# Row sums on one Trainium2 core: the first load becomes a whole group of 16 rows per partition

## The chip, the cores and the metric

The kernel runs on one core of one Trainium2 chip. The metric is device time in microseconds (us): the median of the timed runs. Times inside the kernel come from one profiled execution, counted from its first instruction.

## The reference

```python
batch, seq, dim = 32, 512, 1024
# x: (32, 512, 1024) float32
np.sum(x, axis=-1)          # -> (32, 512) float32
```

16384 rows of 1024 numbers are each summed to one number: 67.1 MB are read and 0.07 MB written.

## The kernel before

**Layout.** The 16384 rows are spread over 128 partitions, 128 rows for each. They lie in two regions: region A, the first 2048 rows, holds 16 rows per partition, and region B holds the other 112 per partition. In each, the rows of one partition are contiguous in memory. `rows_from(j, n)` names rows j to j+n-1 of all partitions. `BIG` is 16 rows per partition, a group of 8.39 MB (64 KB in each partition), so there are 8 groups, 0 to 7; group 0 is region A. `last` is 7 and `tail` is 112, the first row of the last group. `FIRST` is 8.

**Loads.** There are three buffers of 16 rows per partition. The first load is the first eight rows of the last group (4.19 MB, 32 KB per partition). It goes to buffer 0 by SP's queue (L97), and `issue_first_load_at_entry` moves its instruction to the very start of the program, ahead of the barrier that the other engines pass. Groups 0 to 6 follow on POOL's queue (L99), 8.39 MB each, to buffers 1, 2, 0, 1 and so on. The first two of them wait for nothing. Each later one waits until `summed` shows that the reduction of the load three places earlier has ended, which frees the buffer. The prediction numbers loads from 0 (the first one), so load 3 is the first that waits. The last eight rows of the last group are loaded in four runs (two into buffer 2, two into `ends`) behind the same kind of wait.

**Sums.** DVE takes the loads in the order of their issue: for each it waits for the landing and runs one `tensor_reduce` (`vec`, L106), which raises `summed`. The last full group is shared: ten rows go to DVE (`halves`, L115) and six to ACT (`act`, L135). The runs of the last eight rows follow in the same manner. ACT stores the sums that are ready early (L210, L211), and SP the last ones (L227), once DVE and ACT are done.

**Order.** No scheduler takes part: each engine runs its instructions as the program gives them, and only semaphores tie them together. SP issues one load and the last store, POOL all other loads, so a wait on POOL also holds the loads behind it.

Of the kernel before, what the change touches and what calls it, by code (L numbers as in the profile page):

```python
# [30 lines left out]
def kernel(  # L31
# [5 lines left out]
    nc = tc.nc  # L37
# [12 lines left out]
    BIG = 16  # L50
# [15 lines left out]
    def rows_from(j, n):  # L66
        if j < ONE:
            return x_a[:, j : j + n, :]
        return x_b[:, j - ONE : j - ONE + n, :]

    last = J // BIG - 1
    tail = last * BIG
    FIRST = 8

    bufs = [
        ctx.enter_context(nc.sbuf_tensor(f"rows_{k}", [P, BIG * dim], fp32))
        for k in range(3)
    ]
# [9 lines left out]
    def semaphore(name):  # L88
        return ctx.enter_context(nc.semaphore(name=name))

    def block_of(t, a, n):
        return t[:, a * dim : (a + n) * dim].rearrange("p (n d) -> p n d", d=dim)

    def load(dst, src, k):
        sem = semaphore(f"load_{k}")
        if k == "first":
            nc.sync.dma_start(out=dst, in_=src).then_inc(sem, 16)  # L97
        else:
            nc.gpsimd.dma_start(out=dst, in_=src, single_packet=True).then_inc(sem, 16)  # L99
        return sem  # L100

    summed = semaphore("summed")
# [40 lines left out]

    t = bufs[0]
    block = block_of(t, 0, FIRST)
    landed = load(block, rows_from(tail, FIRST), "first")
    loads = [(landed, tail, block)]
    for g in range(last):  # L150
        t = bufs[(1 + g) % 3]
        if g > 1:
            nc.gpsimd.wait_ge(summed, g - 1)
        block = block_of(t, 0, BIG)
        loads.append((load(block, rows_from(g * BIG, BIG), g), g * BIG, block))

    j = tail + FIRST
    t = bufs[(1 + last) % 3]
# [25 lines left out]
    landed, first, block = loads[-1]  # L188
# [70 lines left out]
```

## Time and profile before

| | |
|---|---|
| median of 3 timed runs | 160.72 us (160.71 to 160.88) |
| profiled execution, first to last instruction (its span) | 159.6 us |
| median less span (what lies around the span) | 1.1 us |
| DVE busy | 121.6 us (76% of the span) |
| ACT busy | 11.0 us (7%) |
| POOL busy | 6.2 us (4%) |
| read from memory | 67.11 MB, 421 GB/s over the span |
| packets of POOL's queue (q0) | 62.92 MB, 91.2% of 16 engines' span |
| packets of SP's queue (q1) | 4.20 MB, 6.6% |
| one reduction of 16 rows / of 8 rows | 17.22 us / 8.69 us |

The page gives the span as the profiled execution's own time; the timed runs are other executions, and their median is 1.1 us above it. Sums over stages are made against the span, and the 1.1 us is added at the end. "Busy" of an engine is time in instructions; a DMA issue counts as busy on POOL while the instruction is handled, not while bytes move. A DMA queue's line gives packets, MB and the time of its packets as a share of what 16 DMA engines have. The row "16 rows / 8 rows" is the duration of `tensor_reduce` on 128 partitions by 16384 or 8192 numbers.

### The profile page before, as it was taken

What the parts mean: (1) busy time and instruction counts of PE and PEld (TensorE: products, weight loads), DVE (VectorE), ACT (ScalarE), POOL (GpSimd) and SP (SyncE); (2) the same over time, 40 slices, a digit from 0 to 9 for tenths busy, and PEclk for the clock granted to TensorE, in tenths of its full rate; (3) what the DMA queues carried; (4) which work ended last, traced back from release to release, by engine and by line L of the source; (5) the groups of instructions that cost most, each with busy time, mean ns of one, the idle gap of its engine ahead of it and who ended that gap; (6) DMA issues with size and microseconds to landing.
All of it is one profiled execution on the core that took longest, in us unless ns stands there. A gap on an engine that the chain in (4) does not pass through costs nothing.

```text
span 159.6 us, 123 instructions
## 1 busy us (share of the span) xinstructions
DVE 121.6 (76%) x42; ACT 11.0 (7%) x19; POOL 6.2 (4%) x15
## 2 busy tenths in 40 slices
DVE  0000008999998999949999499986999679995986
ACT  3000000000000000000000000000000000000995
POOL 3000000010001000010000100010000220000000
DMA  7999996996997979969969969969969979898993
GB/s 263 526 394 394 435 600 279 526 509 279 526 444 345 526 345 444 526 279 509 526 263 526 526 263 526 509 279 526 509 279 526 460 329 526 378 411 364 438 402 127
DMA packets 2000, 67.18 MB, mean 421 GB/s; under 512 B 624, under 2 KB 624, under 8 KB 848
## 3 DMA queue, kind: packets, MB, share of 16 engines
q0 software_dynamic: 1424, 62.92, 91.2%
q1 hardware_dynamic: 288, 4.20, 6.6%
q10 hardware_dynamic: 288, 0.06, 0.2%
HBM read 67.11 MB, written 0.07 MB: 421 GB/s over the span
## 4 chain that ended last, share of the span: by engine, by line
DMA 74%; DVE 22%; POOL 1%; issue 1%; POOLq 0%
DMA rows<-in_x_dram 56%; DVE sums L106 22%; DMA ends<-in_x_dram 19%; POOL rows L99 1%; DVE ends L115 0%; DVE sums L115 0%; POOLq L43 0%
## 5 line engine op out<-in xcount | busy, mean ns | idle before, releaser
L106 DVE TENSOR_REDUCE sums<-rows 128x16 f32<-128x16384 f32 (+1 forms) x7 | 111.9, 15999 | 32.2 <-DMA rows<-in_x_dram 32.2
L135 ACT ACTIVATE unread<-rows 128x1024 f32<-128x1024 f32 x9 | 9.1, 1013 | 145.5 <-DMA rows<-in_x_dram 145.5
L115 DVE CUSTOM_DVE_ANT_0 rows<-rows 128x512 f32<-128x512 f32 (+2 forms) x15 | 9.0, 659 | 2.6 <-DMA rows<-in_x_dram 2.6
L99 POOL DMA_DIRECT2D rows<-in_x_dram x9 | 4.9, 546 | 122.4 <-DVE sums L106 120.9
L135 ACT ACTIVATION_READ_ACCUMULATOR unread<-rows 128x1 f32 x9 | 1.7, 186 | 0.0
L135 ACT ACT_TABLE_LOAD x1 | 1.3, 1283 | 1.4 <-PEq L43 1.4
L170 DVE MEMSET ends<- 128x2 f32 x1 | 0.1, 60 | 1.5 <-PEq L43 1.5
L115 DVE DVE_READ_ACCUMULATOR2_ANT sums<- 128x1 f32 x15 | 1.2, 80 | 0.0
L99 POOL DMA_DIRECT2D ends<-in_x_dram x2 | 1.1, 543 | 0.0
L115 DVE CUSTOM_DVE_ANT_0 ends<-ends 128x271 f32<-128x271 f32 (+1 forms) x2 | 0.7, 364 | 0.1
L115 DVE DVE_READ_ACCUMULATOR2_ANT ends<- 128x1 f32 x2 | 0.2, 84 | 0.0
L243 POOL MEMSET const-float32-0.0<- 128x1 f32 x1 | 0.1, 99 | 0.2 <-issue 0.2
L243 POOL MEMSET const-bfloat16-1.0<- 128x1 bf16 x1 | 0.1, 103 | 0.0
L243 POOL MEMSET const-float32-1.0<- 128x1 f32 x1 | 0.1, 99 | 0.0
L243 POOL MEMSET const-uint8-127<- 128x1 uint8 x1 | 0.1, 99 | 0.0
## 6 DMA issues: line engine op xcount, KB each, us to landing
rows<-in_x_dram SPq DMA_DIRECT2D x1, 4096.0 KB, 24.5
rows<-in_x_dram POOLq DMA_DIRECT2D x1, 2802.0 KB, 27.9
rows<-in_x_dram POOLq DMA_DIRECT2D x1, 899.0 KB, 29.6
ends<-in_x_dram POOLq DMA_DIRECT2D x1, 270.0 KB, 29.7
ends<-in_x_dram POOLq DMA_DIRECT2D x1, 125.0 KB, 29.5
rows<-in_x_dram POOLq DMA_DIRECT2D x7, 40.5
out_dram<-sums ACTq DMA_DIRECT2D x1, 48.0 KB, 1.6
out_dram<-sums ACTq DMA_DIRECT2D x1, 8.0 KB, 1.5
```

The lines of the kernel that those rows point to most:

```text
L99: nc.gpsimd.dma_start(out=dst, in_=src, single_packet=True).then_inc(sem, 16)
L106: return nc.vector.tensor_reduce(out=sums[:, j : j + n], in_=block, axis=mybir.AxisListType.X, op=mybir.AluOpType.add,)
L115: return nc.vector.tensor_tensor_reduce(out=src[:, :n], in0=src[:, :n], in1=src[:, n:], scale=1.0, scalar=0.0, op0=mybir.AluOpType.add, op ...
L135: nc.scalar.activation(out=unread[n_acts % len(unread)][:, :], in_=src, func=mybir.ActivationFunctionType.Copy, accum_out=sums[:, j : j + ...
L170: nc.vector.memset(ends[:, six - 1 :: whole8.shape[-1]], 0.0)
L243: nc = _bacc.Bacc("TRN2", target_bir_lowering=False, num_devices=1)
```

## The change

The order of the first two loads is turned round. The first load, on SP's queue and at the program's entry, is now group 0, all 16 rows per partition of region A (8.39 MB, 64 KB per partition), into buffer 0. The eight rows of the last group (4.19 MB) come second, first on POOL's queue, into buffer 1. Groups 1 to 6 follow on POOL's queue, with the same buffers, and each waits for the reduction three places earlier, as before. DVE reduces in the new order: 16 rows, 8 rows, then 16 rows each. The last full group and the runs of the last eight rows are as before.

```diff
-    t = bufs[0]
-    block = block_of(t, 0, FIRST)
-    landed = load(block, rows_from(tail, FIRST), "first")
-    loads = [(landed, tail, block)]
-    for g in range(last):
-        t = bufs[(1 + g) % 3]
-        if g > 1:
-            nc.gpsimd.wait_ge(summed, g - 1)
-        block = block_of(t, 0, BIG)
-        loads.append((load(block, rows_from(g * BIG, BIG), g), g * BIG, block))
+    parts = [(0, BIG), (tail, FIRST)] + [(g * BIG, BIG) for g in range(1, last)]
+    loads = []
+    for k, (first, n) in enumerate(parts):
+        if k > 2:
+            nc.gpsimd.wait_ge(summed, k - 2)
+        block = block_of(bufs[k % 3], 0, n)
+        loads.append((load(block, rows_from(first, n), k or "first"), first, block))
```

The instructions of each engine in the changed program are the same in number: SP's load now has 16384 numbers per partition instead of 8192, POOL's first load 8192 instead of 16384, and DVE's first two reductions change places.

## The prediction

> **What bounds the kernel now.** I read the chain of waits first, then the busy time by stretch, then the start of the timeline, then the packets of each DMA queue. The chain (start, length, what):
>
> ```profile
> 2.61 48.45 DMA rows<-in_x_dram
> ...
> 68.60 40.51 DMA rows<-in_x_dram
> ...
> 127.69 29.73 DMA ends<-in_x_dram
> ```
>
> Between these stand two reductions that the chain crosses because each releases a buffer, but the transfers behind them never stop. The busy time by stretch shows it (length, busy time of DVE, ACT and POOL, clock, share of the 16 DMA engines, GB/s):
>
> ```profile
> 7.20:24.08 16.88, 0.00 (x0) 0.00 (x0) 0.00 (x0) 1.00 1.00 435
> 24.08:50.65 26.57, 25.81 (x2) 0.00 (x0) 0.59 (x2) 1.00 1.00 434
> 51.08:70.43 19.35, 17.22 (x1) 0.00 (x0) 0.57 (x2) 1.00 1.00 434
> 70.43:89.78 19.35, 17.22 (x1) 0.00 (x0) 0.53 (x1) 1.00 1.00 434
> ```
>
> The DMA share is 1.00 in each. An 8.39 MB group takes 19.35 us to move and 17.22 us to sum. So transfers bound the kernel: 67.1 MB at 434 GB/s is 154.6 us of the span's 159.6, and the rest is the start of the first transfer, the sums behind the last one and the last store. A change of order costs something only if it leaves the DMA engines idle; a gap of d us there ends the kernel d us later.
>
> The timeline of the first third (start, length, what, idle before):
>
> ```profile
> 1.94 1.20 POOL L99 DMA_DIRECT2D rows<-in_x_dram  x2 [1.50 <-POOLq L43]
> 24.48 25.81 DVE L106 TENSOR_REDUCE sums<-rows 128x8 f32<-128x8192 f32 x2 [22.91 <-DMA rows<-in_x_dram]
> 33.46 0.53 POOL L99 DMA_DIRECT2D rows<-in_x_dram  x1 [30.31 <-DVE sums L106]
> 50.59 0.53 POOL L99 DMA_DIRECT2D rows<-in_x_dram  x1 [16.60 <-DVE sums L106]
> 51.08 17.22 DVE L106 TENSOR_REDUCE sums<-rows 128x16 f32<-128x16384 f32 x1 [0.79 <-DMA rows<-in_x_dram]
> ```
>
> Three loads can be in flight, one per buffer. The fourth (load 3, issued at 33.46) waits for the first reduction. What had been issued by then keeps the engines busy until load 2 lands at 51.06, so load 3 is issued 17.6 us before it is needed. That cover is what the change spends.
>
> Last, the packets of the two queues from 0 to 6.5 us, and then from 6.5 to 24.1 us (counted where they start):
>
> ```profile
> DMA  0000009995000000099904000999040099904000
> DMA packets 64, 2.10 MB, mean 323 GB/s; under 512 B 0, under 2 KB 0, under 8 KB 0
> q1 hardware_dynamic: 64, 2.10, 85.9%
> ```
>
> ```profile
> DMA packets 176, 8.39 MB, mean 477 GB/s; under 512 B 16, under 2 KB 16, under 8 KB 16
> q0 software_dynamic: 96, 6.29, 82.5%
> q1 hardware_dynamic: 80, 2.10, 27.6%
> ```
>
> Until 6.5 us only SP's queue (q1) moves: four bursts of 16 packets of 32 KB, though POOL issued its loads from 1.94 to 3.14. From then on each of the 16 engines starts six 64 KB packets of POOL's queue (q0) and SP's four remaining ones: packet about, one and one, whatever their sizes. The other 16 packets of q1 are the 4-byte signals.
>
> **The change, part by part.** Bytes, instructions and waits are the same in number: SP issues one load, POOL eleven, DVE runs seven reductions. What moves is which load stands first, and on which queue.
>
> *When the first load lands.* A unit of 32 KB on one engine is 19.35 / 16 = 1.21 us. Before, SP's load is done after its 8 units and the 5 POOL packets of 2 units that fall between them (the sixth begins as the signals go): 18 units, 21.8 us; it lands at 24.48, so start-up and signal take 2.7. After, SP's 8 packets are of 64 KB (16 units), and the POOL packets between them are those of the eight-row load, of 1 unit. If SP has m packets alone at the start, 8 - m are left, with 9 - m POOL packets about them (before: m = 4, 4 left, 5 about them). So it lands at 2.7 + 1.21 x (16 + 9 - m): 30.5 for m = 2, 29.3 for m = 3, 28.1 for m = 4. m = 2 is the same time alone as now; more is possible if an engine lines up several packets ahead.
>
> *When load 3 is issued.* The first reduction is now the long one (17.22), and POOL issues 0.28 after it: 30.5 + 17.5 = 48.0 (m = 2), 46.8 (m = 3), 45.6 (m = 4), instead of 33.46. The queue behind POOL's wait holds only later loads, each of which waits for a later reduction anyway.
>
> *When it is needed.* The same 21.0 MB lie ahead of it, so load 2 still lands at about 51.06. Its last packet ends some 0.4 before that (the first load's signals go at 24.1, its landing is at 24.48), and a burst is spread over some 0.6 us (four slices of 0.16 us above), so the 16 engines run dry one by one from 50.05 to 50.65. The cover shrinks from 17.6 us to 2.0 to 2.6 (m = 2), 3.2 to 3.8 (m = 3) or 4.4 to 5.0 (m = 4).
>
> *What the issue costs.* No row shows how soon POOL's packets move after an issue to an idle queue. Lower bound: the instruction itself, 0.53. Upper bound: the first software packet, 6.55 - 1.94 = 4.6. SP's own load is nearest in kind: issued at 0, first packets at 1.0. How to read the 4.6 decides:
> - An engine takes whatever is ready when a packet ends. Then POOL's packets became ready only after the fourth bursts had begun: 4.0 to 4.6 after the issue, and m = 2. Load 3 is ready at 52.0 to 52.6, and the engines are idle for 1.4 to 2.6 us; a fresh start adds about 0.7 (the 2.7 of the first load, less 1.0 to the first packet and 1.0 of skew and signal). At most +3.3.
> - It lines up packets ahead. With one ahead, they were ready 2.8 to 3.4 after the issue and m = 3: load 3 is ready by 50.2, just in time. With two or three, 0.7 to 2.2 and m = 3 or 4: ready by 49.0, over 1 us early, no gap.
> - It reads ahead by bytes, 32 KB: m = 2 with 2.8 to 3.4, ready at 50.8 to 51.4: a gap of 0.2 to 1.4.
>
> I take a latency of 1 to 2 us, since 0.53 for the instruction and the 1.0 of SP's load are the nearest rows, and with it no gap: 0, with 3.3 as the other end. Nothing here gains: the first packet starts at the same 1.0 us.
>
> The Trainium skill, "DMA: Bandwidth & Descriptors", section "Anatomy of one DMA", puts the fixed part of a GpSimd-issued DMA, completion included, at about 2.0 us. By it, an estimate, load 3 would be ready at 50.0 at the latest even for m = 2, and the sum would be 0; no run here shows that figure.
>
> *What is late next.* DVE starts later, at 30.5 at the latest, and then has landed data for a while: first reduction to 47.8, eight rows to 56.5, load 2 to 73.7, load 3 (landed at 70.4) to 90.9, load 4 (landed at 89.8) to 108.1; load 5 lands at 109.1, as before. DVE has caught up, because it gains 2.13 us per group. The issues in between (56.8, 74.0, 91.2, 108.4) each come while a load of 19.35 us has nearly all of its bytes to go; from load 5 on every time is that of before. ACT, the last runs and the stores follow unchanged.
>
> Sum: 159.6 + 0 for the span; 1.1 us lie around it (160.72 median of the runs less 159.6). Prediction: 160.7.
>
> **The rivals.**
> *The queue runs dry (slower).* Load 3's late issue leaves a hole of 0.4 to 3.3 us at about 50.5: 161.1 to 164.0. It decides from a latency above the cover, 2.0 to 2.6 us with m = 2. For: the 4.6 us of the first issue. Against: that time is also explained by packets lined up, and the first issue is the only one of 0.67 instead of 0.53, so it may not speak for later ones.
>
> *DVE keeps POOL from writing its descriptors (slower).* Load 3 is issued just as DVE begins the eight-row reduction, and landed data keeps DVE busy behind it. If descriptors waited until 56.5, packets would move at some 57.5, 6.9 us after the engines ran dry: 167.6. Against it: the issue at 33.46 fell into a reduction as well and took the same 0.53, and the reduction goes at 17.22 us / 16384 = 1.05 ns an element. But that issue had 17 us of cover, so a delay would not have shown. The Trainium skill, "SBUF — State Buffer", section "SBUF: two separate sides", has the rule behind this: a VectorE op in a two-port fast mode locks GpSimd out of SBUF, and its descriptors wait. It would matter only if these reductions ran in that mode, which no row names.
>
> *SP's load does not go as 64 KB packets.* It moved 32 KB ones so far. Cut in two, it is 16 packets: 4 alone, 12 left with 13 POOL packets about them, 8 of one unit and 5 of two: 34 units, landing at 43.8. Load 3 is issued at 61.3, over 10 us after the engines ran dry: 12 us more with the latency, some 173. Against: POOL's loads already go as 64 KB packets.
>
> *Faster.* Only the start could give anything, if 64 KB packets start with less than the 0.6 us between engines: 160.3.
>
> **How the numbers follow.** A measurement of this kernel can tell about 0.2% (0.3 us). No gap: 0.56, within 0.2%. The queue runs dry: 0.30; DVE lock: 0.04; cut packets: 0.05; together slower 0.39. Faster: 0.05. The range takes in the first two cases and the bounds of the latency: 160.5 to 164.0, with 0.09 above it and 0.04 below; the likeliest case alone is 160.5 to 161.0.
>
> **What would show it.** Right: the first DVE reduction has 16 rows and starts at 28 to 30.6; POOL issues its third load at 45.6 to 48.1; the stretch from 50 to 53 us moves 434 GB/s without a pause; the third reduction ends near 73.7 and waits of 2.13 us come back from load 5 on. Wrong: a start near 44 (cut packets); a dip in the DMA share at 50.5 and load 3 landing after 70.4; an issue of over 0.53 us, or packets that start when a reduction ends. The forecast falls if load 3's first packets come over 2.6 us after its issue.

## The result, and the profile after

| | before | after |
|---|---|---|
| median of 13 runs each | 160.68 us | 161.28 us |
| range | 160.52 to 160.88 | 160.73 to 161.69 |
| profiled execution: its time, and its span | span 159.6 | 161.45, span 160.1 |

The ratio is 1.0036, 95% interval 1.0029 to 1.0043: slower by 0.6 us, which is more than the 0.2% that a measurement of this kernel can tell. The runs are also spread wider, 0.96 us against 0.36.

The chain of waits of the changed kernel (start, length, what):

```profile
0.00 30.31 DMA rows<-in_x_dram
30.31 0.02 issue
30.34 42.95 DVE sums L106 x3
73.29 0.28 issue
73.57 36.16 DMA rows<-in_x_dram
```

The first load lands at 30.31 and DVE sums three loads without a pause, to 73.29. The transfer that follows (load 5) lands at 109.73; before, the same load landed at 109.11. So 0.62 us were lost ahead of it, and what comes behind runs at the old pace, as the timeline shows (start, length, what, idle before; lines between are left out at the dots):

```profile
47.85 0.53 POOL L99 DMA_DIRECT2D rows<-in_x_dram  x1 [44.71 <-DVE sums L106]
56.44 0.53 POOL L99 DMA_DIRECT2D rows<-in_x_dram  x1 [8.07 <-DVE sums L106]
...
109.75 17.22 DVE L106 TENSOR_REDUCE sums<-rows 128x16 f32<-128x16384 f32 x1 [2.13 <-DMA rows<-in_x_dram]
```

POOL's first issue here is load 3, at 47.85. The wait of 2.13 us is back at load 5. The packets of the first 6.4 us:

```profile
DMA packets 32, 2.10 MB, mean 328 GB/s; under 512 B 0, under 2 KB 0, under 8 KB 0
q1 hardware_dynamic: 32, 2.10, 86.4%
```

32 packets of 64 KB on 16 engines: SP has two packets alone (m = 2), and they are whole, not cut in two. In the trace POOL's first packets start at 6.50.

Where the 0.62 us lie is seen at load 3. The profile's row of its DMA issue gives the time from issue to landing (the last number, us), first for the changed kernel and the issue at 47.85:

```profile
rows<-in_x_dram POOLq DMA_DIRECT2D x1, 23.2
```

Then for the kernel before and the issue at 33.46:

```profile
rows<-in_x_dram POOLq DMA_DIRECT2D x1, 37.0
```

By these rows it lands at 47.85 + 23.2 = 71.05 instead of 33.46 + 37.0 = 70.46; the trace has 71.04 and 70.41. This is so although load 2 lands at 50.87 (trace), 0.2 earlier than before. Between the two landings lie 20.17 us instead of 19.35.

The trace shows how. Call the first 64 KB packet of load 3 on each of the 16 engines a first packet. No pause is seen: in order of time, the sixteen first packets start from 50.01 to 50.49, each within 0.02 us of one of load 2's sixteen 4-byte signals, which start from 50.00 to 50.48. But four of them, which start from 50.29 to 50.49, take 2.48, 2.68, 2.76 and 3.30 us, where 64 KB packets otherwise take 2.42 (the few others over 2.45 us between 31 and 127 us take 2.46 to 2.69). So the loss is a longer first packet on some engines. The engine that lost 0.88 us here stays late to the end: at each load from 3 to 7 the last of the 16 signals comes 0.72 to 0.73 us behind the one before it, against 0.23 to 0.28 in the kernel before.

### The profile page after: what moved, and what is told of

It is laid out like the page before. It is cut to its first block, busy times and chain, and to the rows that moved or that the text cites. A ratio compares the mean times of both kernels' runs of the same rounds, so it can differ in the third digit from the quotient of the medians.

```text
span 160.1 us, 123 instructions
## 1 busy us (share of the span) xinstructions
DVE 121.4 (76%) x42; ACT 11.0 (7%) x19; POOL 6.1 (4%) x15
## 4 chain that ended last, share of the span: by engine, by line
DMA 60%; DVE 38%; POOL 1%; issue 1%
DMA rows<-in_x_dram 42%; DVE sums L106 38%; DMA ends<-in_x_dram 19%; POOL rows L99 1%; DVE ends L115 0%; DVE sums L115 0%
```

## The experiments

Three theories were set against each other. T: the cover of load 3 is too thin, since its packets do not follow soon enough on its issue. L: DVE's reductions hold up the descriptors that POOL writes. O: the order itself, with 64 KB packets at the start, makes the engines uneven. When T's size did not fit, it was replaced by U: behind engines that are still busy an issue needs longer, up to some 3.7 us, until its packets follow at full pace. An engine "runs dry" where its last packet of load 2 ends. Each ratio is against the kernel before, timed beside that run on the same chip.

**The changed order, load 3 issued early.** ACT sums six rows of the first group beside DVE's ten:

```diff
-        vec(first, block).then_inc(summed, 1)
+        vec(first, block[:, :n_dve, :]).then_inc(summed, 1)   # n_dve = 10 for the first load, else all
+        for q in range(n_dve, block.shape[1]):
+            act(first + q, block[:, q, :], landed if q == n_dve else None)
...
+        if k == 3:
+            nc.gpsimd.wait_ge(acts, 6)
```

> The changed order, but ACT sums six of the first group's 16 rows, so that DVE ends its ten rows some 6.3 us earlier and POOL issues load 3 near 41.5 us instead of 47.85. Theory T (thin cover: POOL's packets need 2 to 3.4 us from the issue, and the engines run dry from 49.9 to 50.4): the cover is 8.5 us, no packet of load 3 takes longer than 2.42 us, load 3 lands 19.35 us after load 2 (20.2 in the changed kernel), and the time is that of before, 160.5 to 160.7. Theory L (DVE's reductions hold up POOL's descriptors): DVE is busy at the issue too, so some of the loss stays unless the cover hides it: 160.6 to 161.3. Theory O (the order itself, with 64 KB packets on SP's queue at the start, makes the engines uneven, whenever load 3 is issued): 161.3 as in the changed kernel.

Measured: issue at 41.51, load 3 lands 19.35 us after load 2, no first packet over 2.45 us, 160.73 us, ratio 1.0006 (0.9997 to 1.0014). Load 2 lands at 50.94 here, and load 3 at 41.51 + 28.8 = 70.3:

```profile
rows<-in_x_dram POOLq DMA_DIRECT2D x1, 28.8
```

The loss is gone with the order unchanged, so O falls.

**The old order, load 3 issued late.** POOL's load 3 also waits for 14 of the second load's 16 rows:

```diff
+        if i == 1:
+            vec(first, block[:, :14, :]).then_inc(late, 1)
+            vec(first + 14, block[:, 14:, :]).then_inc(summed, 1)
+            continue
...
+        if g == 2:
+            nc.gpsimd.wait_ge(late, 1)
```

> The old order (eight rows first on SP's queue), but POOL's load 3 also waits until DVE has summed 14 of the second load's 16 rows, so it is issued near 48.2 us instead of 33.46, about as late as in the changed kernel (47.85). The engines run dry from 50.05 to 50.65. T: packets of load 3 take up to 1 us longer on some engines, load 3 lands 0.3 to 1.3 us late, time 161.0 to 162.0. L: the same as T, since DVE sums the last two rows while POOL writes descriptors. O: the old order keeps the old time, 160.7.

Measured: issue at 48.40, 14 of 16 first packets between 2.51 and 3.01 us, load 3 lands 19.79 us after load 2, 161.03 us, ratio 1.0021 (1.0013 to 1.0030). The issue, and the row that gives the landing (48.40 + 22.1 = 70.5, load 2 at 50.75):

```profile
48.40 0.53 POOL L99 DMA_DIRECT2D rows<-in_x_dram  x1 [45.27 <-DVE sums L107]
```

```profile
rows<-in_x_dram POOLq DMA_DIRECT2D x1, 22.1
```

The loss appears in the old order as well: the lateness of the issue brings it.

**DVE idle at the issue.** DVE waits for load 2 before its second reduction:

```diff
+        if i == 1:
+            nc.vector.wait_ge(loads[2][0], 16)
```

> The changed order, but DVE waits for load 2 (near 51 us) before its second reduction, so it is idle from 47.6 to 51 while POOL issues load 3 at the same 47.85. By the durations of the trace DVE still catches up before the last group. T: the loss is that of the changed kernel, 161.1 to 161.5, load 3 lands 20.0 to 20.4 us after load 2. L: the loss goes, 160.7, load 3 lands 19.35 us after load 2. O: 161.3.

Measured: 161.06 us (160.71 to 161.59), ratio 1.0021 (1.0009 to 1.0032); the profiled run was among the quickest, with two first packets of 2.49 and 2.57 us and load 3 19.40 us after load 2. The median lay between the theories, so this kernel was run again beside the changed kernel on the same chip:

> The changed kernel as it is, run again beside the next one, for a comparison on one chip. All theories: 161.1 to 161.4, ratio near 1.0036 to before.

> The changed order with DVE idle from 47.6 to 51 us, again, now beside the changed kernel itself. On an idle queue first packets took 2.57 to 3.27 us with DVE idle and 2.87 to 3.93 with DVE at work, so DVE at work may add some 0.3 us to a thin cover. If so: 0.2 to 0.4 us below the changed kernel, 160.8 to 161.0. If DVE plays no part (U): the same as the changed kernel within 0.15.

Measured: 161.15 us, ratio 1.0030 (1.0016 to 1.0045), for the changed kernel, and 161.24 us, ratio 1.0035 (1.0022 to 1.0049), with DVE idle. The profiles agree: the changed kernel has seven long first packets of up to 2.99 us and load 3 lands 19.88 us after load 2; with DVE idle it is five of up to 3.10 us, and 19.93. The loss is there without DVE's work, so L falls as its cause; a part of it below some 0.2 us could not be told in these runs.

**An idle queue.** Load 3 waits for the second reduction too:

```diff
-            nc.gpsimd.wait_ge(summed, k - 2)
+            nc.gpsimd.wait_ge(summed, max(k - 2, 2))
```

> The changed order, but load 3 waits for the second reduction too (issue near 56.4 us instead of 47.85), with the engines idle since 50.4 and DVE at work on the next group. It measures the time from POOL's issue to the first packets on an idle queue. T: first packets 2 to 3.4 us after the issue, 58.4 to 59.8; the engines idle for 8 to 9.4 us, time 168.7 to 170.5. A latency of 1 to 2 us, as the prediction took it: packets at 57.4 to 58.4, time 168 to 169. L: packets only when the reduction of load 2 ends near 73.5, time over 183.

Measured: one run of 169.41 us. The timeline gives the issues of load 3 and load 4, and the busy time by stretch shows that no packet starts before 57.6:

```profile
56.45 1.04 POOL L99 DMA_DIRECT2D rows<-in_x_dram  x2 [53.30 <-DVE sums L106]
```

```profile
50.30:57.60 7.30, 7.30 (x2) 0.00 (x0) 1.04 (x2) 1.00 0.00 0
57.60:62.00 4.40, 4.40 (x1) 0.00 (x0) 0.00 (x0) 1.00 1.32 477
```

In the trace the first packet starts at 57.67, 1.22 us after the issue, and the sixteen first packets take 2.87 to 3.93 us instead of 2.42. So, by an estimate (1.22 plus the 0.45 to 1.51 that a first packet took longer), bytes run at full pace some 1.7 to 2.7 us after the issue. DVE was at work all this time, from 50.3 on.

The same with DVE idle meanwhile (DVE waits for load 3 before it sums load 2):

> As the run with the dry queue (load 3 waits for the second reduction, issue near 56.4 us), but DVE waits for load 3 before it sums load 2, so DVE is idle while POOL writes the descriptors and the packets start. T: as with DVE at work: first packets 1.2 us after the issue, each 0.45 to 1.5 us longer than 2.42. L (DVE at work slows POOL's descriptors): packets clearly sooner than 1.2 us after the issue, or first packets of 2.5 to 2.9 instead of 2.9 to 3.9. The time, 170 to 185, says nothing by itself, since DVE then runs late.

Measured: first packets 1.23 us after the issue and 2.57 to 3.27 us long; 176.29 us, of which DVE's wait is the reason. The start is the same. The packets were somewhat shorter, in one profile each; the two runs above, made because of it, show no effect on the time.

**How much cover is enough.** The changed order, with one, two or three rows of the first group on ACT (the first diff with n_dve 15, 14 and 13), or with one row summed once more, so that the issue moves in steps of 1.05 to 1.2 us:

> The changed order, ACT sums one of the first group's 16 rows, so POOL issues load 3 near 46.8 us, 1.05 earlier than in the changed kernel: cover 3.1 to 3.6 us instead of 2.1 to 2.6. Theory T, now with its size (first packets 1.2 us after the issue on an idle queue, and 0.45 to 1.5 us more for a first packet that follows an empty queue, so 1.7 to 2.7 in all): no loss but for a rare outlier, 160.6 to 160.8. Theory O (the order itself): 161.1 to 161.3. A half-way result, 160.9 to 161.0, would say that a tail of the latency reaches beyond 3 us.

> The changed order, but DVE sums one row of the first group once more into a spare column before its reduction, so POOL issues load 3 near 48.95 us, 1.1 later than in the changed kernel: cover 1.0 to 1.5 us. T: all engines wait, by 0.2 to 1.7 us, the last of them by about 1: load 3 lands 20.3 to 21 us after load 2, time 161.7 to 162.3. If the loss did not depend on the cover (O): 161.1 to 161.4.

> The changed order, ACT sums two of the first group's 16 rows, so POOL issues load 3 near 45.85 us: the engines run dry 4.2 to 4.7 us later. With one row on ACT (issue 46.92, 3.2 to 3.7 before dry) the loss had not gone (161.11), against theory T. Theory U: an issue behind engines that are still busy needs longer until its packets follow without a pause than one on an idle queue, up to some 3.7 us, as POOL's first issue did at the start (4.5 us to its first packet, beside SP's load). U: most of the loss goes, 160.65 to 160.85, and few or no packets of load 3 over 2.45 us. If the loss has nothing to do with the cover between 42 and 47 us but with the work that ACT took over, it goes in proportion: 161.0.

> The changed order, ACT sums three of the first group's rows: issue near 44.8 us, 5.3 to 5.8 before the engines run dry, beyond the 4.5 us that POOL's first issue took. U: no packet of load 3 over 2.45 us, load 3 lands 19.35 us after load 2, 160.6 to 160.75. In proportion to ACT's share: 160.9.

Measured, with the other runs of this order, by the time of the issue. The engines run dry from some 49.9 to 50.6 in all of them (the 4-byte signals behind load 2, in the traces). "Long" counts the first packets that took over 2.45 us. The runs with two and three rows were timed on another chip than the other experiments.

| rows on ACT | issue | load 2 to load 3 landing | long, of 16 | median us | ratio (95%) |
|---|---|---|---|---|---|
| one summed twice | 49.03 | 20.22 | 16 | 161.64 | 1.0059 (1.0047 to 1.0071) |
| 0 (the change) | 47.85 | 20.17 | 4 | 161.28 | 1.0036 (1.0029 to 1.0043) |
| 1 | 46.92 | 19.46 | 3 | 161.11 | 1.0031 (1.0020 to 1.0041) |
| 2 | 45.72 | 19.36 | 0 | 160.75 | 1.0007 (0.9998 to 1.0016) |
| 3 | 44.65 | 19.35 | 0 | 160.83 | 1.0015 (1.0006 to 1.0025) |
| 6 | 41.51 | 19.35 | 0 | 160.73 | 1.0006 (0.9997 to 1.0014) |

An issue 3.0 to 3.7 us ahead of the dry engines still loses half a microsecond in the median, one 4.2 to 4.8 ahead nothing that can be told. Theory T with 1.7 to 2.7 us expected no loss at 46.92 and is wrong in size. U was made to fit that run; the run with two rows was its test, and it passed. Two things limit this. The profile with one row on ACT, of a quick run (160.95 us), shows only 0.11 us lost at load 3. And the step from one row to two is also a step from one chip to another; on one chip alone the bounds are 3.0 to 3.7 us (loss) and the 8.6 to 9.0 of six rows (none). The landing of the two neighbours, each from the row of its DMA issue: with one row on ACT, 46.92 + 23.6 = 70.5,

```profile
rows<-in_x_dram POOLq DMA_DIRECT2D x1, 23.6
```

and with two, 45.72 + 24.5 = 70.2:

```profile
rows<-in_x_dram POOLq DMA_DIRECT2D x1, 24.5
```

The run with three rows is inconclusive as to its 0.18 us (U expected 160.75 at most): load 3 loses nothing there, but over 70 packets of 2.45 to 2.67 us are strewn from 81 to 145 us in its profile, long after this issue, and loads 6 and 7 take 19.44 and 19.69 us instead of 19.35. So time is also lost elsewhere now and then, and why is open.

The latest issue, at 49.03, shows the start itself. Its first packets begin at 50.25, again 1.22 us after the issue, though the first engine ran dry only at 49.94; all sixteen take 2.77 to 3.44 us.

**Another queue.** Load 3 and all loads behind it go on SP's hardware queue:

```diff
-        if k == "first":
+        if k not in (1, 2):
             nc.sync.dma_start(out=dst, in_=src).then_inc(sem, 16)
...
-            nc.gpsimd.wait_ge(summed, k - 2)
+            nc.sync.wait_ge(summed, k - 2)
```

> The changed order, but load 3 and everything behind it goes on SP's hardware queue instead of POOL's; load 3 is issued at the same time, near 47.8 us. T: what counts is the time from issue to bytes. SP's first load had packets 1.0 us after its issue, and its first packets took 0.1 to 1.05 us longer than later ones, so 1.1 to 2.05 in all, just within the cover of 2.1 to 2.6: load 3 lands 19.35 to 19.6 us after load 2, time 160.5 to 161.0 unless the small last runs go worse on this queue. O: 161.3.

Measured: 161.56 us (160.97 to 162.19), ratio 1.0056 (1.0037 to 1.0075), against the expectation. Load 3 was issued at 47.44 and landed 19.88 us after load 2, and all 16 first packets were long, 2.66 to 3.00 us. The row of the issue, 47.44 + 23.2 = 70.6 (load 2 landed at 50.73):

```profile
rows<-in_x_dram SPq DMA_DIRECT2D x1, 23.2
```

A change of queue does not buy the cover back. POOL does not issue this load, so the loss here cannot come from descriptors that POOL is kept from writing, which speaks against L once more. In that profile the rest runs at the old pace; why other runs are up to 1.1 us slower still was not followed.

No run was faster than the kernel before: the best of them only give back the cover that it has.

## Why the prediction was wrong

Its forecast was no change. The first rival, "The queue runs dry", 161.1 to 164.0 with a chance of 0.30, comes nearest, at its lower end, though not as the hole that it described: the engines went on without a pause, and some first packets were long.

- *Bound by transfers, and a gap of d us ends the kernel d us later*: right. The 0.62 us lost at load 3 stand unchanged at load 5, and the medians differ by 0.60. The 1.1 us that the sum put around the span are 1.3 in the changed kernel (161.45 less 160.1); the forecast does not hang on it.
- *When the first load lands*: right. m = 2 gave 30.5; it was 30.31.
- *When load 3 is issued*: 48.0 forecast for m = 2, 47.85 measured. *When it is needed*: 50.05 to 50.65 forecast, some 50.0 to 50.5 in the trace.
- *What the issue costs*: this step failed. It took "a latency of 1 to 2 us" and set only that against the cover of 2.0 to 2.6. As the time to the first packet that was well placed (1.22 us), and the packets did start in time, 2.16 to 2.64 us after the issue. Two things were missing. The 0.7 us of a fresh start was added only behind a gap, but first packets take 0.45 to 1.5 us longer on an idle queue, so 1.7 to 2.7 us had to fit into the cover already. And behind engines that are still busy even 3.0 to 3.7 us did not do. The term was set at 0 and measured 0.6 us. Why a first packet takes longer when its issue is recent stays open.
- *How to read the 4.6 us*: of its three readings, a latency of 1 to 2 us goes only with two or three packets lined up ahead by number, and so with m = 3 or 4. That was shown wrong by the changed kernel's own start: m is 2, and POOL's packets come at 6.50 after two packets of 64 KB, as they came at 6.54 after four of 32 KB. This start does not tell the two other readings apart, since two packets of 64 KB are as many bytes as four of 32 KB and take about as long. The reading by bytes gave a gap of 0.2 to 1.4 us, which holds the measured loss; the reading of 4.0 to 4.6 us gave 1.4 to 2.6 and does not. As a time to the first packet neither carries over to load 3, whose first packets came 2.16 us after the issue at 47.85. That the cover which the sweep asks for (over 3.0 to 3.7, at most 4.2 to 4.8) is near 4.6 us is not shown to have the same reason.
- *The fixed part of 2.0 us* (the Trainium skill, "DMA: Bandwidth & Descriptors", section "Anatomy of one DMA"): by it, an estimate, the sum was 0. On the idle queue 1.7 to 2.7 us to full pace and some 0.4 for the signal (29.94 to 30.31 at the first load) come near it; behind busy engines it is too short. The same page of the Trainium skill, "DMA: Bandwidth & Descriptors", section "Latency and other measured facts", gives memory access as 0.2 us on average and 2 us at high load. That would go with a longer way under load, but no run here shows which part of the way grows.
- *What is late next*: right, nothing; DVE ended its third reduction at 73.3 (73.7 forecast).
- *DVE keeps POOL from writing its descriptors*: shown wrong. POOL's packets start 1.22 us after an issue amid DVE's work, not after the reduction, and an idle DVE changes nothing in the time that can be told (161.24 us against 161.15). The lock of which the Trainium skill speaks ("SBUF — State Buffer", "SBUF: two separate sides") did not show with these reductions.
- *Cut packets* and *faster*: neither happened.

The size is also a matter of chance from run to run: how many first packets are long, and by how much, differs between runs of one kernel (four of up to 3.30 us in one profile of the change, seven of up to 2.99 in the other). This may be part of why its runs spread over 0.96 us, but it is not shown: the two profiled runs took nearly the same time (161.45 and 161.49), with 0.82 and 0.53 us lost between loads 2 and 3, because in the second load 2 already landed 0.28 us later. What makes a single engine's packet late was not found.

## What to carry to other kernels

When a change delays a load's issue, do not compare what is left of its cover only with the length of the issue or the time to the first packet (here 1.22 us): count the longer first packet too. Better, move the issue in steps, as here, and see where the loss ends; in this kernel some 4 us of queued transfers were needed and 2.1 to 2.6 were left. Look at the length of the first packets as well as at pauses. This kernel, bound by transfers, can keep a long first reduction if part of it goes to an idle engine: two rows on ACT were enough.

## What the runs showed of the hardware

- A POOL load issued to idle engines has its first packet after 1.22 to 1.23 us, and its first 64 KB packets take 2.57 to 3.93 us instead of 2.42.
- One issued 2.1 to 2.6 us before the engines run dry starts its packets without a pause, but 4 of 16 first packets were long, by up to 0.88 us; with 3.0 to 3.7 us still 3 of 16 were, by up to 0.45. SP's hardware queue does no better: with 2.5 to 2.9 us left, every first packet took 0.24 to 0.58 us longer.
- An engine that falls behind does not catch up while transfers follow one another: in the changed kernel the last of the 16 signals stays 0.72 to 0.73 us behind the one before it from load 3 to load 7.
- Two queues share an engine packet by packet whatever the size: 64 KB of SP's against 32 KB of POOL's here, 32 against 64 before. From 6.4 to 29.45 us, until SP's load was nearly done, each engine of the changed kernel started six packets of SP's queue and seven of POOL's.
